# Low parts of eight weight tiles made by accumulating DMAs, three renormalisations fewer per table, and looser buffers in a hybrid SSM/attention encoder block

## The chip, the cores and the metric

One core of one Trainium2 chip runs the whole program. The metric is the device time of one execution in microseconds (us), the median of the runs. A core has five engines with queues of their own, which run in order and wait for one another by semaphores: TensorE (PE), VectorE (DVE), ScalarE (ACT), GpSimd (POOL) and SyncE (SP). DMAs are issued by SP, ACT and POOL.

## The reference

One encoder layer (DEPTH 1) over 512 tokens and 16 meta tokens, width 1024, all in float32:

```python
h = rms_norm(h_res, norm_mix_g[i])
proj = h @ w_in[i]
u, q, k, v, g_ssm, g_attn = jnp.split(proj, split_at, axis=-1)
y = s5_bidirectional(u, ...)                  # 32 groups, 64 complex states, both directions
z = jax.nn.gelu(y, approximate=False)
y_ssm = z * jax.nn.sigmoid(z @ w_glu[i] + b_glu[i])
...                                           # q, k: per-head norm and rotary; attention
merged = (jax.nn.sigmoid(g_ssm) * (y_ssm @ w_ssm_proj[i])
          + jax.nn.sigmoid(g_attn) * (y_attn @ w_attn_proj[i]))
h_res = h_res + merged @ w_out[i]
h2 = rms_norm(h_res, norm_mlp_g[i])
h_res = h_res + jnp.square(jax.nn.relu(h2 @ w_mlp_in[i])) @ w_mlp_out[i]
```

One direction of the S5 part is a complex diagonal recurrence x_t = lb x_(t-1) + B u_t, followed by Re(C x). What the change touches lies in this part and in the projections that run beside it.

## The kernel before, in words

**Precision.** Each float32 operand of a dense product is split into a high part (a copy rounded to fp32r) and a low part (the operand less its high part), and `mm3` (L157 to L161) does three matmuls: high x high (L159), low x high and high x low (L160, L161, the order depends on which side the weights are).

**Weights.** `load_w` (L107) fetches 512 KB into `wf` by a DMA on SP's queue (L112), ScalarE copies it into `wh` in two halves (L98), and the low part `wl` is made in one of two ways. Either VectorE subtracts, in two halves (L125), or, where the second entry of `W_ENG` is None, ScalarE writes the negated copy into `wl` (L122) and a DMA on GpSimd's queue adds `wf` to it (L123, `accum_op=ALU.add`). The tiles `wf`, `wh` and `wl` have two buffers each. The second way is in use before the change in the MLP stage alone.

**The state stage** runs from about 56 us to 234 us. VectorE prepares the parameters of the recurrence. Then there are eight passes of four groups each, i8 = 0 to 7 (pass 0 to pass 7 below). `ssm_build` makes the pass's matrices: the transposed input matrices (VectorE products L711 to L713 in `tmp`, PE transposes `w` L720), the output matrices `W2` (VectorE L728 to L733, two buffers), the phase table `e` from two products in `x1` and `x2` (L747) and their sum (L749), and the small Toeplitz part (PE `kt` L758, then `T0` by eight small DMAs). `ssm_run` does the pass: PE `st` (L787), ScalarE copies into `Sx` (L789, L790), on VectorE a rotation (L795 to L797), a scan (L800) and a rotation back, on ScalarE the copies into `X` (L806, L807), and PE `yo` (L813 with `T0`, L815 with `X` and `W2`). `m1` of the rotation lies in `rs1`, the same store as `x1`, so that the next pass's `x1` cannot be written before the copies into `X` have read `m1`.

**Filler.** Between the steps of the passes PE is given the matmuls of fourteen projection tasks: u columns (`t_u`, 48 matmuls of 264 columns into `ups`) and gate columns (`t_gate`, 24 matmuls of 512 columns into `gps`). Each task loads one weight tile with `load_w`, one task ahead. The first eight tiles of the stage are called load 1 (the task u1), load 2 (the gate g0), load 3 (g1) and so on. The instructions of each engine are put in order when the program is built, by a list scheduler with priorities; that order is then fixed.

**Phase tables.** `phase_tables` builds powers of the unit phase by doubling. After each squaring (`csq`) it calls `renorm`, six VectorE instructions on 128x32 values, which brings the modulus back to one.

Of the kernel before, what the change touches and what calls it, by code (L numbers as in the profile page):

```python
# [10 lines left out]
F32 = mybir.dt.float32  # L11
# [59 lines left out]
def hybrid_block(ctx, tc, x, meta, w_in, w_glu, w_ssm, w_attn, w_out, w_m1, w_m2,  # L71
# [20 lines left out]
    W_ENG = [lambda i: (S, Q if i % 2 else V)]  # L92
# [391 lines left out]
    x_st.close()  # L484
    fill_q += [kv_t[0], t_u(0, uTs), kv_t[1]]
    drain()
    W_ENG[0] = lambda i: (S, V)


    def tt(a, b, op, o=None):  # L490
# [83 lines left out]
    def csq(r, i):  # L574
        rr = tz(tz(r, r, ALU.mult), tz(i, i, ALU.mult), ALU.subtract)
        ii = stt(r, 2.0, i, ALU.mult, ALU.mult, o=ptile(ppz))
        return rr, ii

    def renorm(r, i):
        m = tz(tz(r, r, ALU.mult), tz(i, i, ALU.mult), ALU.add)  # L580
        m = ts(m, -0.5, ALU.mult, 1.5, ALU.add, o=ptile(ppz))
        return tz(r, m, ALU.mult), tz(i, m, ALU.mult)
# [7 lines left out]
    def phase_tables():  # L590
        wr, wi = wri
        phase = []
        for nb in (8, 9):
            tr_ = sp.tile([128, G, nb], F32, name=f"ph{nb}r")
            ti_ = sp.tile([128, G, nb], F32, name=f"ph{nb}i")
            V.memset(tr_[:, :, 0:1], 1.0)
            V.memset(ti_[:, :, 0:1], 0.0)
            m = 1
            while m < nb:
                n = min(m, nb - m)  # L600
                bcw = [a[:, :, None].to_broadcast([128, G, n]) for a in (wr, wi)]
                s1, s2 = [a[:, :G * n].rearrange("p (g n) -> p g n", g=G) for a in (sc5, sc6)]
                cmul(V, tr_[:, :, m:m + n], ti_[:, :, m:m + n], tr_[:, :, 0:n], ti_[:, :, 0:n], bcw[0], bcw[1], s1, s2)
                m *= 2
                if m < nb or nb == 8:
                    wr, wi = renorm(*csq(wr, wi))
            phase.append((tr_, ti_))

        (pbr, pbi), (par, pai) = phase
        pa1, pa2 = [sp.tile([128, G, 2, 9], F32, name=f"pa{j}") for j in range(2)]  # L610
        S.copy(out=pa1[:, :, 0], in_=par)
        S.copy(out=pa1[:, :, 1], in_=pai)
        S.activation(out=pa2[:, :, 0], in_=pai, func=AF.Copy, scale=-1.0)
        S.copy(out=pa2[:, :, 1], in_=par)
        return pa1, pa2, pbr, pbi
# [79 lines left out]
    def ssm_build(i8):  # L695
# [46 lines left out]
        e = sw.tile([128, 4, 2, 72], F32, tag="e", name="e")  # L742
        es = sw.tile([128, 2, 4, NC], F32, tag="es", name="es")
        E4 = [128, 4, 18, 8]
        x1, x2_ = [a.rearrange("p (g a b) -> p g a b", g=4, b=8) for a in (rs1, rs2)]
        for o, a, b_ in ((x1, pa1, pbr), (x2_, pa2, pbi)):
            V.tensor_tensor(out=o, in0=a[:, gs].rearrange("p g s a -> p g (s a)")[:, :, :, None].to_broadcast(E4),  # L747
                            in1=b_[:, gs, None, :].to_broadcast(E4), op=ALU.mult)
# [27 lines left out]
    def ssm_run(i8, ws_, Uf):  # L776
        W1T, W2, T0, er, es = ws_
        gs = slice(4 * i8, 4 * i8 + 4)
        b = i8 % 2
        SX = [128, 2, 4, NC]  # L780
        S.copy(out=dec[:, :, :, 1:], in_=m8[:, None, gs, None].to_broadcast([128, 2, 4, NC - 1]))

        Sx = sw.tile(SX, F32, tag="S", name="Sx")
        for i in range(2):
            ps = ptr("st")[:, :4 * NC].rearrange("p (g n) -> p g n", g=4)
            for g in range(4):
                own = PE.matmul(out=ps[:, g, :], lhsT=W1T[i][:, g, :], rhs=Uf[:, 4 * b + g, :], start=True, stop=True)  # L787
            anchors.append(own.ins)
            S.copy(out=Sx[:64, i], in_=ps[:64])  # L789
            S.copy(out=Sx[64:, i], in_=ps[64:, :, ::-1])  # L790
        m1, m2_ = [a[:, :8 * NC].rearrange("p (i g n) -> p i g n", i=2, g=4) for a in (rs1, rs2)]
        erb = er[:, None].to_broadcast(SX)

        def rotate(op):
            V.tensor_tensor(out=m1, in0=Sx, in1=erb, op=ALU.mult)  # L795
            V.tensor_tensor(out=m2_, in0=Sx[:, ::-1], in1=es, op=ALU.mult)
            marks[1] = V.tensor_tensor(out=m1, in0=m1, in1=m2_, op=op).ins  # L797
        fl_ = [a.rearrange("p i g n -> p (i g n)") for a in (Sx, dec, m1)]
        rotate(ALU.add)
        V.tensor_tensor_scan(out=fl_[0], data0=fl_[1], data1=fl_[2], initial=0.0, op0=ALU.mult, op1=ALU.add)  # L800
        rotate(ALU.subtract)

        xf = sw.tile(SX, F32, tag="X", bufs=XB, name="X")
        Q.memset(xf[:64, :, :, 0:1], 0.0)  # L804
        Q.memset(xf[64:, :, :, NC - 1:NC], 0.0)
        S.copy(out=xf[:64, :, :, 1:], in_=m1[:64, :, :, :NC - 1])  # L806
        S.copy(out=xf[64:, :, :, NC - 2::-1], in_=m1[64:, :, :, :NC - 1])  # L807
        Xn = [xf[:, i] for i in range(2)]
        yield

        ps = ptr("yo")[:NCR].rearrange("n (g f) -> n g f", g=4)
        for g in range(4):
            PE.matmul(out=ps[:, g, :], lhsT=Uf[:, 4 * b + g, c0:], rhs=T0[:, g, :], start=True, stop=False)  # L813
            for i in range(2):
                own = PE.matmul(out=ps[:, g, :], lhsT=Xn[i][:, g, c0:], rhs=W2[i][:, g, :], start=False, stop=i == 1)  # L815
        anchors.append(own.ins)
        marks[0] = copy_on(S, Ysb[:, :, 4 * b:4 * b + 4, :], ps.rearrange("n g (t p) -> n t g p", t=T)).ins
# [760 lines left out]
```

## Time and profile before

| | |
|---|---|
| median of 3 runs | 918.15 us (916.77 to 918.69) |
| profiled execution | 916.32 us, its span 914.6 us |
| busy, share of the span | PE 93%, DVE 76%, ACT 56%, POOL 20% |
| mean granted TensorE clock | 0.976 |
| chain that ended last | PE 76%, DVE 14%, ACT 5% |
| accumulating DMAs | 27, all after 590 us |

Times are microseconds from the start of the span. A row of the timeline gives start, duration, engine, line, operation, output and inputs, and in brackets how long the engine had been idle before it and who released it. Instructions of one engine overlap a little at their ends, so what one costs is the distance to the next start. The granted clock is a share of 2.4 GHz; the lower of its two levels is 1.2 GHz.

### The profile page before, as it was taken

The numbers are of one execution on the slowest core, as the hardware profiler recorded it, in microseconds if no ns is written. First come the engines' busy times: TensorE is split into PE (matmuls) and PEld (weight loads), VectorE is DVE, ScalarE is ACT, GpSimd is POOL, SyncE is SP. The second block draws the span as 40 slices with busy tenths as digits, with TensorE's granted clock in tenths as the row PEclk, the third lists the DMA queues.
The fourth block names the chain that finished last, engine by engine and source line by source line (L and its number), as shares of the span: only waits on it lengthen the run. The fifth ranks groups of instructions, "written<-read, shape, count | busy, mean of one in ns | idle before, by whom it ended". The sixth has DMA issues, their size and how long they took to land.

```text
span 914.6 us, 13094 instructions
## 1 busy us (share of the span) xinstructions
PE 852.6 (93%) x4798; PEld 729.8 (80%) x4798; DVE 691.2 (76%) x1263; ACT 515.9 (56%) x908; POOL 184.4 (20%) x177
## 2 busy tenths in 40 slices
PE   6999789998999899899989999999999999999994
PEld 5998677776887789788878888888888888888884
DVE  6999999878879687867685536747667666776687
ACT  5444465555663656578785335565655555555543
POOL 1000000000111476657644432010010001000000
PEclk9999899899999999999999999999999999999997
DMA  7222202222113110002014343565656566565402
GB/s 236 71 67 67 75 13 63 75 58 65 63 47 95 50 47 24 24 24 70 2 48 137 115 138 92 187 161 138 183 138 161 140 181 153 147 180 127 109 1 92
DMA packets 96322, 88.33 MB, mean 97 GB/s; under 512 B 4337, under 2 KB 79665, under 8 KB 96258
## 3 DMA queue, kind: packets, MB, share of 16 engines
q1 hardware_dynamic: 87824, 69.25, 25.2%
q0 software_dynamic: 4016, 14.21, 7.9%
q10 hardware_dynamic: 4418, 4.04, 1.6%
q8 instruction: 38, 0.62, 0.3%
q14 instruction: 26, 0.21, 0.1%
HBM read 69.03 MB, written 2.10 MB: 78 GB/s over the span
## 4 chain that ended last, share of the span: by engine, by line
PE 76%; DVE 14%; ACT 5%; issue 2%; DMA 1%; POOL 1%; DVEq 0%; ACTq 0%; POOLq 0%
PE m L161 6%; PE m L160 6%; PE m L159 6%; PE o L159 5%; PE o L160 5%; PE o L161 5%; PE pv L1173 3%; PE sc L1099 2%; PE atr L1123 2%; DVE wl L125 2%; PE adp L159 2%; PE adp L160 2%; PE adp L161 2%; PE gps L159 2%; PE kt L758 2%
## 5 line engine op out<-in xcount | busy, mean ns | idle before, releaser
L98 ACT CAST wh<-wf 128x512 fp32r<-128x512 f32 (+1 forms) x120 | 89.8, 778 | 94.5 <-PE m L160 58.2
L1444 DVE TENSOR_TENSOR ybuf<-o,ybuf 128x1024 f32<-128x1024 f32 x52 | 63.5, 1221 | 67.9 <-PE o L161 67.8
L161 PE MATMUL m<-h2h,wl 128*128 128x512 f32 (+1 forms) x272 | 102.4, 377 | 0.8 <-DVE wl L125 0.8
L160 PE MATMUL m<-h2l,wh 128*128 128x512 f32 (+1 forms) x272 | 102.5, 377 | 0.2 <-DVE h2l L103 0.2
L159 PE MATMUL m<-h2h,wh 128*128 128x512 f32 (+1 forms) x272 | 102.3, 377 | 0.3 <-ACT h2h L98 0.2
L160 PE MATMUL o<-ol,fh 128*128 128x512 f32 (+1 forms) x216 | 83.2, 385 | 0.0
L159 PE MATMUL o<-oh,fh 128*128 128x512 f32 (+1 forms) x216 | 83.2, 385 | 0.0
L161 PE MATMUL o<-oh,fl 128*128 128x512 f32 (+1 forms) x216 | 83.2, 385 | 0.0
L125 DVE TENSOR_TENSOR wl<-wf,wh 128x512 fp32r<-128x512 f32 (+1 forms) x81 | 69.2, 873 | 14.1 <-ACT wh L98 13.3
L123 POOL DMA_DIRECT2D wl<-wf x27 | 23.4, 866 | 279.0 <-ACT wl L122 262.3
L161 PEld LDWEIGHTS m<-h2h,wl 128*128 128x128 f32 x272 | 51.2, 188 | 10.6 <-DVE wl L125 1.3
L159 PEld LDWEIGHTS m<-h2h,wh 128*128 128x128 f32 x272 | 51.1, 188 | 10.1 <-ACT h2h L98 0.5
L160 PEld LDWEIGHTS m<-h2l,wh 128*128 128x128 f32 x272 | 51.2, 188 | 9.7 <-DVE h2l L103 0.4
L1103 DVE TENSOR_REDUCE mx<-sc 128x1 f32<-128x528 f32 x64 | 44.7, 701 | 11.7 <-PE sc L1099 10.8
L103 DVE TENSOR_TENSOR pl<-atr,ph 128x512 fp32r<-128x512 f32 x64 | 43.4, 683 | 9.3 <-ACT ph L98 8.5
L98 ACT CAST ph<-atr 128x512 fp32r<-128x512 f32 x64 | 37.1, 584 | 18.1 <-PE atr L1123 17.5
L161 PEld LDWEIGHTS o<-oh,fl 128*128 128x128 f32 x216 | 40.6, 188 | 8.2
L159 PEld LDWEIGHTS o<-oh,fh 128*128 128x128 f32 x216 | 40.6, 188 | 8.1
L160 PEld LDWEIGHTS o<-ol,fh 128*128 128x128 f32 x216 | 40.6, 188 | 7.9
L804 POOL MEMSET X<- 64x8 f32 x8 | 0.9, 112 | 218.4 <-PE yo L815 218.4
L1113 POOL TENSOR_TENSOR ea<-zT,rsm 128x528 f32<-128x528 f32 x32 | 34.2, 1069 | 21.4 <-DVE rsm L1112 19.3
L1123 PE MATMUL atr<-ident,ea 128*128 128x128 f32 x192 | 36.0, 281 | 0.7 <-DVE pl L103 0.6
(403 smaller groups left out, 2523.4 us busy)
## 6 DMA issues: line engine op xcount, KB each, us to landing
wf<-in_w_in_dram SPq DMA_DIRECT2D x32, 512.0 KB, 3.9
wf<-in_w_m_dram SPq DMA_DIRECT2D x32, 512.0 KB, 4.1
q<-in_w_m_dram SPq DMA_DIRECT2D x32, 512.0 KB, 4.5
wl<-wf POOLq DMA_DIRECT2D x27, 512.0 KB, 4.4
ybuf<-in_x_dram SPq DMA_DIRECT2D x8, 512.0 KB, 3.9
wf<-in_w_attn_dram SPq DMA_DIRECT2D x8, 512.0 KB, 3.9
wf<-in_w_out_dram SPq DMA_DIRECT2D x8, 512.0 KB, 3.3
wf<-in_w_ssm_dram SPq DMA_DIRECT2D x4, 512.0 KB, 3.4
```

Of the source, the lines that this page charges most:

```text
L98: return S.copy(out=o, in_=i)
L103: b = el.tensor_tensor(out=l, in0=src, in1=h.bitcast(F32), op=ALU.subtract)
L123: Q.dma_start(out=wl[:, r], in_=wf[:, r], accum_op=ALU.add)
L125: el.tensor_tensor(out=wl[:, r], in0=wf[:, r], in1=wh[:, r].bitcast(F32), op=ALU.subtract)
L159: PE.matmul(out=o, lhsT=lh, rhs=rh, start=first, stop=False, skip_group_check=goes_on)
L160: PE.matmul(out=o, lhsT=lh, rhs=rl, start=False, stop=False, skip_group_check=goes_on)
L161: return PE.matmul(out=o, lhsT=ll, rhs=rh, start=False, stop=last, skip_group_check=goes_on)
L1103: g0 = V.tensor_reduce(out=mx, in_=sc[:, :, :NL], axis=AX.XY, op=ALU.max, negate=True)
L1113: pend.append(lambda: Q.tensor_tensor(out=en, in0=e, in1=rs_.to_broadcast([128, L]), op=ALU.mult))
L1123: PE.transpose(ps[:, j * 256 + q * 128:j * 256 + q * 128 + 128], ea[2 * f + q][:, c:c + 128], ident)
L1173: PE.matmul(out=pvt[0][:, 256 * f:256 * f + 256], lhsT=vw, rhs=pw, start=left == [8, 9], stop=left == [0, 0])
L1444: V.tensor_tensor(out=x2q[r][h], in0=z, in1=x2q[r][h], op=ALU.add)
```

## The change

It has four parts. The low parts of the state stage's first eight weight tiles are made by ScalarE's negated copy and an accumulating DMA, no longer by VectorE. `renorm` is called once, at the end of the first phase table, where it was called after each of six squarings: five calls go. `x1` moves from `rs1` to a free part of `yfl`. `Sx` gets two buffers.

```diff
-    W_ENG[0] = lambda i: (S, V)
+    nw0 = wcount[0]
+    W_ENG[0] = lambda i: (S, V if i - nw0 > 7 else None)
...
-                    wr, wi = renorm(*csq(wr, wi))
+                    wr, wi = csq(wr, wi)
+                    if m == nb:
+                        wr, wi = renorm(wr, wi)
...
-        x1, x2_ = [a.rearrange("p (g a b) -> p g a b", g=4, b=8) for a in (rs1, rs2)]
+        x1, x2_ = [a.rearrange("p (g a b) -> p g a b", g=4, b=8) for a in (yfl[:, 3072:3648], rs2)]
...
-        Sx = sw.tile(SX, F32, tag="S", name="Sx")
+        Sx = sw.tile(SX, F32, tag="S", bufs=2, name="Sx")
```

From `nw0` on the changed kernel's line numbers are one larger, from the `renorm` lines on three larger.

The scheduler puts the instructions in another order. At the start of the stage, where load 1 becomes the weights of the task u1 (`ups`), PE has this before:

```order
L161 MATMUL kvps<-wh,hTl 16x256
L159 MATMUL ups<-hTh,wh 128x264
L160 MATMUL ups<-hTl,wh 128x264
L159 MATMUL ups<-hTh,wh 128x264
L160 MATMUL ups<-hTl,wh 128x264
L161 MATMUL ups<-hTh,wl 128x264
```

And in the changed kernel:

```order
L161 MATMUL kvps<-wh,hTl 16x256
L159 MATMUL ups<-hTh,wh 128x264
L160 MATMUL ups<-hTl,wh 128x264
L159 MATMUL ups<-hTh,wh 128x264
L160 MATMUL ups<-hTl,wh 128x264
L723 MATMUL w_922<-ident,ybuf 128x128 x4
L161 MATMUL ups<-hTh,wl 128x264
```

Four transposes of pass 0 now stand ahead of the first matmul that reads the low part `wl`; before they came 27 matmuls later. ScalarE has this at the same place before (`kvps` is the K/V task that ends there):

```order
L98 COPY kvraw<-kvps 128x256 x2
L98 CAST wh<-wf 128x512 x2
L98 COPY kvraw<-kvps 16x256
L98 CAST wh<-wf 128x512 x2
L721 COPY W_921<-w_922 128x512
```

And in the changed kernel, where the negated copies of loads 1 and 2 stand ahead of their high parts:

```order
L98 COPY kvraw<-kvps 128x256 x2
L122 ACTIVATE wl<-wf 128x1024
L98 CAST wh<-wf 128x512 x2
L122 ACTIVATE wl<-wf 128x1024
L98 COPY kvraw<-kvps 16x256
L98 CAST wh<-wf 128x512 x2
L724 COPY W_921<-w_922 128x512
```

On GpSimd, whose queue held only the zeroing of the edges of `X` in this stage, the accumulating DMAs come in between. This is the piece of the changed kernel from pass 0's zeroing to pass 2's:

```order
L123 DMA wl<-wf 128x1024
L807 MEMSET X 64x8
L808 MEMSET X 64x8
L123 DMA wl<-wf 128x1024 x6
L807 MEMSET X 64x8
L808 MEMSET X 64x8
L123 DMA wl<-wf 128x1024
```

Loads 2 to 7 stand between pass 0's zeroing and pass 1's, load 8 behind pass 1's.

The third place is on VectorE, from the end of pass 2's rotation back (its last product into `gbuf` is the first row) to pass 3's scan. Before:

```order
L797 TENSOR_TENSOR gbuf<-gbuf,rs_888 128x528
L747 TENSOR_TENSOR rs_888<-pa_1116,ph8i 128x576
L747 TENSOR_TENSOR gbuf<-pa_1115,ph8r 128x576
L749 TENSOR_TENSOR e<-gbuf,rs_888 128x576
L731 TENSOR_TENSOR W_1853<-ybuf 128x512
L795 TENSOR_TENSOR gbuf<-Sx,e 128x528
L728 TENSOR_TENSOR ybuf<-Cr,PA_848 128x512
L729 TENSOR_TENSOR ybuf<-Ci,PA_847 128x512
L125 TENSOR_TENSOR wl<-wf,wh 128x512
```

The second half of pass 3's rotation and the second half of the subtraction follow, then more of the next build, and the scan only as the seventh row from there. In the changed kernel:

```order
L800 TENSOR_TENSOR gbuf<-gbuf,rs_888 128x528
L750 TENSOR_TENSOR rs_888<-pa_1056,ph8i 128x576
L752 TENSOR_TENSOR e<-ybuf,rs_888 128x576
L750 TENSOR_TENSOR ybuf<-pa_1055,ph8r 128x576
L798 TENSOR_TENSOR gbuf<-Sx,e 128x528
L799 TENSOR_TENSOR rs_888<-Sx,es 128x528
L800 TENSOR_TENSOR gbuf<-gbuf,rs_888 128x528
L734 TENSOR_TENSOR W_1793<-ybuf 128x512
L125 TENSOR_TENSOR wl<-wf,wh 128x512
L803 SCALAR_TENSOR_TENSOR Sx<-dec,gbuf 128x528
```

One of the two products of the phase table (`x1`, now in `ybuf`) is already made when pass 2 ends, and pass 3 is rotated at once and scanned two instructions later, where products of the next build came in between before.

## Rows read from the trace of the kernel before

**Rows 1.** Stretches of the state stage: length, busy time of each engine (instructions), clock, DMA share.

```profile
60.00:80.00 20.00, 20.00 (x123) 17.05 (x122) 19.88 (x52) 8.12 (x18) 0.00 (x0) 1.00 0.35 94
...
104.00:112.00 8.00, 1.28 (x5) 0.72 (x5) 6.55 (x10) 4.39 (x10) 0.00 (x0) 0.65 0.23 66
112.00:118.00 6.00, 5.25 (x27) 4.66 (x26) 5.75 (x9) 1.94 (x4) 0.21 (x2) 0.62 0.00 0
```

**Rows 2.** Who PE waited for between 95 and 235 us: total, times, longest.

```profile
PE yo L815 <- ACT X L807: 6.6, 3, 3.5
```

**Rows 3.** PE's timeline at the outputs of passes 0, 1, 3, 7, and the stage's end.

```profile
109.45 0.69 PE L813 MATMUL yo<-T,Uf 128*64 128x128 f32 x2 [5.27 <-ACT Sx L790]
111.60 1.09 PE L815 MATMUL yo<-W,X 128*64 128x128 f32 x4 [1.46 <-ACT X L807]
...
123.10 0.60 PE L815 MATMUL yo<-W,X 128*64 128x128 f32 x4
...
159.43 0.71 PE L678 MATMUL ug<-ident,Vc 66*128 66x66 f32 x8 [2.13 <-ACT Vc L98]
161.81 1.09 PE L815 MATMUL yo<-W,X 128*64 128x128 f32 x4 [1.67 <-ACT X L807]
...
228.76 0.65 PE L815 MATMUL yo<-W,X 128*64 128x128 f32 x4 [3.52 <-ACT X L807]
...
229.63 1.06 PE L815 MATMUL yo<-W,X 128*64 128x128 f32 x4
...
234.32 0.50 PE L159 MATMUL adp<-zh,wh 128*128 128x512 f32 x1
```

**Rows 4.** The subtractions of the first eight loads on DVE, 56 to 107 us.

```profile
L125 DVE TENSOR_TENSOR wl<-wf,wh x16: 679/682/693, 56.1 to 105.4; 128x512 fp32r<-128x512 f32 x16
```

**Rows 5.** DVE's timeline: a renorm instruction and its successor, a subtraction and its successor.

```profile
47.89 0.18 DVE L492 TENSOR_TENSOR p<-p 128x32 f32<-128x32 f32 x1
47.99 0.68 DVE L563 TENSOR_TENSOR sc<-p,Bi 128x512 f32<-128x512 f32 x1
...
59.43 0.68 DVE L125 TENSOR_TENSOR wl<-wf,wh 128x512 fp32r<-128x512 f32 x1
60.03 0.68 DVE L711 TENSOR_TENSOR ybuf<-LBi,PA 128x512 f32<-128x512 f32 x1
```

**Rows 6.** The group of x1, 60 to 240 us: busy, mean ns, idle before and releaser.

```profile
L747 DVE TENSOR_TENSOR gbuf<-pa,ph8r 128x576 f32<-128x576 f32 x8 | 6.0, 755 | 4.2 <-ACT X L807 4.2
```

**Rows 7.** The accumulating DMAs of the MLP stage, their landing, the first with its copy.

```profile
L123 POOL DMA_DIRECT2D wl<-wf x27: 860/862/917, 600.6 to 856.0; - x27
DMA to landing us min/median/max: 4.4/4.4/5.7
599.21 1.05 ACT L122 ACTIVATE wl<-wf 128x1024 fp32r<-128x1024 f32 x1
600.57 0.92 POOL L123 DMA_DIRECT2D wl<-wf  x1 [46.09 <-ACT wl L122]
```

**Rows 8.** The start of the stage on ACT and PE, and the first gate matmul.

```profile
54.57 1.14 ACT L98 CAST wh<-wf 128x512 fp32r<-128x512 f32 x2 [1.03 <-PE kvps L161]
56.82 0.39 PE L161 MATMUL ups<-hTh,wl 128*128 128x264 f32 x1
60.33 0.60 PE L720 MATMUL w<-ident,ybuf 128*128 128x128 f32 x4
64.55 0.50 PE L159 MATMUL gps<-hTh,wh 128*128 128x512 f32 x1
```

**Rows 9.** DVE: pass 0's first phase product, the K norm's reduction, pass 7's last rotation step.

```profile
100.53 0.75 DVE L747 TENSOR_TENSOR gbuf<-pa,ph8r 128x576 f32<-128x576 f32 x1
...
202.73 1.49 DVE L917 TENSOR_REDUCE st<-ybuf 128x20 f32<-128x1280 f32 x1 [1.34 <-ACT ybuf L916]
...
226.54 0.70 DVE L797 TENSOR_TENSOR gbuf<-gbuf,rs 128x528 f32<-128x528 f32 x1
```

**Rows 10.** A DMA issue of T0 on ACT's queue: shortest, median, longest.

```profile
L769 ACTq DMA_DIRECT2D T<-gbuf x32: 592/608/1437, 77.3 to 210.1; - x32
```

## The prediction, made before the changed kernel was run

> **What bounds the kernel now.** I read the table of stretches first. Over the whole span PE is busy 93%, so a change pays only where PE stands still or runs at its lower clock. In the state stage both kinds occur. From 60 to 80 us PE and DVE are both full [rows 1]. From 104 to 112 us PE works 1.28 of 8 us, and up to 118 us its granted clock is near 0.62, while DVE is busy 12.3 of these 14 us [rows 1]: the filler has run out and PE waits for pass 0's chain on DVE. The list of PE's waits has 6.6 us in three waits for `X` [rows 2]; ahead of the first of them stand 5.27 us until `Sx` is copied (the copy waits on ACT's queue behind work that waits for DVE). The timeline puts them at passes 0, 3 and 7, and shows the price of the lower clock: a step of four `yo` matmuls takes 1.09 us at 111.60 and 161.81 us and 0.60 us at 123.10 us [rows 3]. A whole `yo` has four such steps, 4 x (1.09 - 0.60) = 2.0 us, so the low level costs it 2.0 us, and a little more with the `T0` matmuls in between.
>
> So DVE bounds the stage in several places and PE in others, above all from 60 to 104 us. DVE work that goes is worth at most PE's idle time; anything that holds PE between 56 and 104 us costs in full.
>
> **What goes.** The sixteen subtractions lie between 56.1 and 105.4 us [rows 4]. One costs 0.60 us, from its start to the next [rows 5]: 16 x 0.60 = 9.6 us. Five `renorm` calls are 30 instructions at 0.10 us [rows 5]: 3.0 us. Both lie ahead of or in pass 0's chain, whose phase product starts at 100.53 us [rows 9]. `x1` in its own store removes DVE's 4.2 us of waiting for the copies into `X` [rows 6]. Two buffers of `Sx` let ACT copy the next pass's input before the rotation back has read the last one. Together DVE gets 9.6 + 3.0 + 4.2 = 16.8 us.
>
> What PE gets from it, place by place:
> - Pass 0: the waits of 5.27 and 1.46 us [rows 3]. DVE reaches the chain about 12 us earlier, more than the 6.7 us, so both go; with PE kept busy `yo` runs at the high level, 2.0 us less, which I round up to 2.3 for the `T0` matmuls. Together 9.0.
> - Pass 3: waits of 2.13 and 1.67 us, and `yo` at the low level from 161.81 us, 2.0: 5.8. The order now rotates pass 3's input (copied early into the second `Sx`) ahead of the next build's products, so I take all of it.
> - Pass 7: 3.52 us, and behind it three of the four steps at the low level (1.06 us at 229.63 us, [rows 3]), 1.5: 5.0. The chain from pass 6's `st` to pass 7's last rotation step at 226.54 us [rows 9] loses little, and the K norm's reduction of 1.49 us [rows 9], which stood in a hole of DVE, now stands inside it, since its square is written over the store that `x1` takes. I take half: 2.5.
>
> The sum is 17.3 us, which agrees with DVE's 16.8. The tasks' matmuls are neither more nor fewer, so whatever filler moves keeps its price.
>
> **What comes in.** Eight negated copies of 1.05 us on ACT [rows 7], which is busy 8.12 of 20 us at 60 to 80 us [rows 1], so their busy time is hidden. Eight DMA issues of 0.86 us on POOL, which is idle there. What counts is how long `wl` takes. From the copy's start: 1.05, then 0.31 until the DMA is issued (599.21 + 1.05 to 600.57 us), then 4.4 to landing [rows 7]: 5.8 us, where the subtraction took 1.3.
>
> - Load 1. The buffer is free when the K/V task ends; ACT's first copy was released at 54.57 us [rows 8]. So `wl` is there at 54.5 + 5.8 = 60.3 us. PE took the first low part at 56.82 us [rows 8]; the four transposes that now stand ahead of it cover at most their 0.60 us [rows 8], I take 0.5. PE stalls for 60.3 - 57.3 = 3.0 us, in the stretch where it is the bound. Pass 0's `kt` and its successors come no later than before, as they now stand ahead of the first gate task.
> - The clock behind that stall. PE lost the high level behind waits of 3.52 us and of 5.27 + 1.46 us [rows 3]; the price was 1.5 and 2.0 to 2.3 us. Behind 3.0 us it lies between 0 and 2.3; I take 1.5, near the upper end, because 3.0 is close to 3.52.
> - Loads 2 to 8. A buffer is freed when its task ends, and PE then has the other task to do. From 64.55 us [rows 8] to the idle before 109.45 us, that is 104.2 us [rows 3], PE does 102 gate matmuls and 48 of `ups` (its order before, from the first `gps` to the first `yo` with `X`), 5.25 tasks, in 39.6 us: 7.5 us each. That covers 5.8 us with 1.7 to spare, provided that ACT is free. It is not always: in the new order load 4's copy stands behind four DMA issues of `T0`, 0.6 us each [rows 10], so I expect about 1 us there and 0.5 elsewhere: 1.5 (bounds 0 and 7 x 3.0 = 21).
> - On POOL pass 1's zeroing stands behind the DMA of load 7. By the walk above that DMA is issued near 106 us and the zeroing needs pass 0's `yo` anyway, so it is covered; a later load 7 would hold pass 1's `X` by as much.
> - DVE now runs ahead and meets another wait: pass 2's `W2` needs the buffer that pass 0's `yo` reads. Behind that instruction pass 1's scan is queued, and PE's next `yo` waits for it with what filler is left. I take 1.0 on PE; the bounds are 0 and the longest wait for `X` now, 3.52 us [rows 3].
>
> Costs: 3.0 + 1.5 + 1.5 + 1.0 = 7.0. Net gain 17.3 - 7.0 = 10.3 us. The profiled execution of 916.32 us (span 914.6) becomes 906.0 (span 904.3). It is 1.83 us under the median of the runs, so the median goes from 918.15 to 907.8 us.
>
> **A rule against it.** The 27 landings of the MLP stage lie between 4.4 and 5.7 us, median 4.4, although DVE works there beside them [rows 7]. The state stage's DVE is fuller (19.88 of 20 us, [rows 1]). The Trainium skill's page "SBUF — State Buffer" (section on the two separate sides, the box on DVE blocking a DMA) says that a DMA issued from GpSimd has its descriptors written by GpSimd, and that VectorE locks it out while it runs an instruction in a two-port performance mode, for which an fp32 copy from SBUF to SBUF is the example. By that rule landings would be late only beside such copies; DVE's work between 56 and 106 us is nearly all tensor_tensor products, the kind that ran beside the landings of 4.4 us. If DVE did hold the DMAs, each would take the longest landing, 5.7 - 4.4 = 1.3 us more, and with no cover 8 x 1.3 = 10.4 us would use up the gain: 918.
>
> **The rivals.**
> 1. Slower: `wl` is late for every load. It decides when ACT starts the negated copy more than 1.7 us after the buffer is free, on the mean of the eight. For it: ACT's queue is in order, and copies that wait for PE or DVE and the `T0` issues stand ahead. Against it: ACT is busy 8 of 20 us there [rows 1]. Price: 8 x 3.0 = 24 in place of 4.5, the rest as above: 24 + 1.5 + 1.0 - 17.3 = 9 us slower, 927.
> 2. The gain stays at pass 0: later waits keep their length because DVE is tied to PE by the two buffers of `W2` and by the single `X`. Then 9.0 - 7.0 = 2 us, 916. For it: POOL's and DVE's instructions for `X` and `W2` wait for `yo`, so no pass can run far ahead. Against it: the order at pass 3 has the rotation ahead of the build's products.
> 3. The rule above holds: 918.
> 4. All covers hold: 17.3 - 3.0 and the rest of pass 7, 2.5: 17 us faster, 901.
>
> **How the numbers follow.** Forecast (6 to 15 us faster, 903 to 912): 0.63. Rival 1: 0.13. Rival 2: 0.17. Rival 3: 0.04. Rival 4: 0.03. What a measurement here can tell from no change is about 0.2%, 1.8 us, near the spread of the three runs. Rival 2 lies at that edge, I give it 0.11 faster and 0.06 same; rival 3 is 0.01 same and 0.03 slower. So faster 0.63 + 0.11 + 0.03 = 0.77, same 0.07, slower 0.16. The range 900 to 920 leaves out most of rival 1 and little else. The forecast's own is 903 to 912.
>
> **What would show it.** Right: a PE wait near 57 us of about 3 us whose releaser is the DMA of `wl`; none of the waits of [rows 3] at passes 0 and 3; clock 1.00 around pass 0's `yo`, which starts near 107 us (111.6 before); landings of L123 near 4.4 us in this stage too; the stage's end (the first `adp` matmul, 234.3 us before) near 224. Wrong: PE waits for `wl` or L123 before every task up to 110 us; landings over 5.7 us; pass 1's `X` held by its zeroing; or, with the early waits gone, the same wait found again at passes 5 to 7.

## The result, and the profile after

The changed kernel takes 905.3 us (median of four runs, 902.95 to 906.97) against 917.9 us for the kernel before in the same runs: a ratio of 0.9862, 95% interval 0.9836 to 0.9887, 12.6 us faster. The profiled execution took 902.95 us with a span of 901.0 us, 13.6 us less than before. (Of the five `renorm` calls that go, two lie in the first phase table and three in the second, so the title's "three per table" holds for the second alone.) Here are PE's waits in it between 45 and 240 us (total, times, longest).

```profile
PE kt L761 <- DVE W L736: 3.9, 2, 2.2
PE yo L818 <- ACT X L810: 1.7, 1, 1.7
PE ups L161 <- DMA wl<-wf: 1.6, 1, 1.6
PE yt L827 <- ACT gbuf L98: 1.5, 2, 0.8
PE kt L761 <- DVE W L734: 1.2, 3, 0.6
PE ups L159 <- ACT kvraw L98: 1.2, 1, 1.2
PE ug L681 <- ACT Vc L98: 1.1, 2, 0.7
PE gps L161 <- DMA wl<-wf: 0.8, 2, 0.5
```

Three waits for `X` with 6.6 us [rows 2] have become one of 1.7. PE's timeline puts them in place, with the same points as [rows 3] and load 1 ahead.

```profile
57.80 0.39 PE L159 MATMUL ups<-hTh,wh 128*128 128x264 f32 x1 [1.22 <-ACT kvraw L98]
60.33 0.39 PE L161 MATMUL ups<-hTh,wl 128*128 128x264 f32 x1 [1.58 <-DMA wl<-wf]
...
106.03 0.65 PE L818 MATMUL yo<-W,X 128*64 128x128 f32 x4
...
151.19 0.65 PE L818 MATMUL yo<-W,X 128*64 128x128 f32 x4
...
186.55 1.73 PE L761 MATMUL kt<-W,BP 128*48 128x128 f32 x14 [2.22 <-DVE W L736]
...
217.41 0.62 PE L818 MATMUL yo<-W,X 128*64 128x128 f32 x4 [1.73 <-ACT X L810]
...
221.31 0.50 PE L159 MATMUL adp<-zh,wh 128*128 128x512 f32 x1
```

The first `adp` matmul comes 13.0 us earlier than in [rows 3], so all but 0.6 of the 13.6 us lie in the state stage. Passes 0 and 3 begin without a wait and at the high level (0.65 us a step); load 1 stalls PE, and two `kt` groups wait for `W2` near 187 and 193 us.

**A ledger of the stage.** Time that PE loses is idle time, and of its busy time the share that the granted clock takes (1 less PEclk). The stretches of the stage in the kernel before (start and end, length, busy time with instructions of PE, PEld, DVE, ACT and POOL, PEclk, DMA share, GB/s):

```profile
54.00:82.00 28.00, 27.79 (x178) 23.80 (x176) 27.83 (x75) 11.73 (x25) 0.00 (x0) 1.00 0.33 85
82.00:138.00 56.00, 46.78 (x311) 40.20 (x309) 51.62 (x126) 32.79 (x68) 0.43 (x4) 0.91 0.18 48
138.00:166.00 28.00, 24.13 (x162) 21.30 (x162) 24.65 (x40) 14.58 (x33) 0.21 (x2) 0.91 0.29 75
...
166.00:234.32 68.32, 61.51 (x372) 51.34 (x370) 57.37 (x97) 37.88 (x75) 0.85 (x8) 0.94 0.22 62
```

And in the changed kernel:

```profile
54.00:82.00 28.00, 25.02 (x164) 21.58 (x163) 26.92 (x81) 15.16 (x29) 3.74 (x6) 1.00 0.55 123
82.00:138.00 56.00, 53.38 (x375) 46.10 (x374) 46.20 (x80) 39.85 (x81) 3.86 (x8) 1.00 0.51 116
138.00:166.00 28.00, 27.58 (x169) 22.36 (x168) 23.86 (x39) 15.52 (x34) 0.43 (x4) 0.94 0.29 77
166.00:221.31 55.31, 48.07 (x316) 40.05 (x314) 47.09 (x77) 32.94 (x66) 0.66 (x6) 1.00 0.20 53
```

Idle time is length less PE's busy time. The clock's share was added up in steps of 1 us, because much of the low clock lies in idle time and costs nothing there: 8.9 us before, 1.7 after. (In the third stretch after, for example, 27.58 us at 0.94 is 1.7.) In us lost:

| stretch | before: idle, clock | after: idle, clock | gained |
|---|---|---|---|
| load 1, 54 to 82 | 0.2, 0 | 3.0, 0 | -2.8 |
| passes 0 and 1, 82 to 138 | 9.2, 2.7 | 2.6, 0 | 9.3 |
| passes 2 and 3, 138 to 166 | 3.9, 2.1 | 0.4, 1.7 | 3.9 |
| 166 to the stage's end | 6.8, 4.1 | 7.2, 0 | 3.7 |
| sum | 20.1, 8.9 | 13.3, 1.7 | 14.0 |

Stage end less 54 us and less both losses is 151.3 us before and 152.3 after, and 150.0 to 152.7 in all fourteen kernels below: PE's own work differs by 2.7 us at most, and how long a kernel's stage is follows from what PE loses in it. The stretches are fixed in time, and the changed kernel is 6 us ahead at pass 2 and 11 at pass 3, so a loss near a border can fall into another one.

### The profile page after: what moved, and what is told of

Same layout as the page of the kernel before. It is cut to its first block, busy times and chain, and to the rows that moved or that the text cites. A ratio compares the mean times of both kernels' runs of the same rounds, so it can differ in the third digit from the quotient of the medians.

```text
span 901.0 us, 13081 instructions
## 1 busy us (share of the span) xinstructions
PE 844.8 (94%) x4798; PEld 721.6 (80%) x4798; DVE 676.2 (75%) x1217; ACT 521.9 (58%) x916; POOL 193.2 (21%) x185
## 4 chain that ended last, share of the span: by engine, by line
PE 74%; DVE 14%; ACT 6%; DMA 3%; issue 3%; POOL 1%; DVEq 0%; ACTq 0%; POOLq 0%; SPq 0%
PE m L161 6%; PE m L160 6%; PE m L159 6%; PE o L161 5%; PE o L159 5%; PE o L160 5%; PE pv L1176 3%; PE sc L1102 2%; PE atr L1126 2%; DVE wl L125 2%; PE gps L159 2%; PE gps L161 2%; PE gps L160 2%; PE adp L159 2%; PE adp L160 2%
## 5 line engine op out<-in xcount | busy, mean ns | idle before, releaser
L123 POOL DMA_DIRECT2D wl<-wf x35 | 30.3, 865 | 377.4 <-ACT wl L122 299.5
L125 DVE TENSOR_TENSOR wl<-wf,wh 128x512 fp32r<-128x512 f32 (+1 forms) x65 | 57.3, 900 | 13.4 <-ACT wh L98 13.2
L161 PEld LDWEIGHTS m<-h2h,wl 128*128 128x128 f32 x272 | 51.2, 188 | 10.5 <-DVE wl L125 1.3
L159 PEld LDWEIGHTS m<-h2h,wh 128*128 128x128 f32 x272 | 51.1, 188 | 10.1 <-ACT h2h L98 0.5
L1106 DVE TENSOR_REDUCE mx<-sc 128x1 f32<-128x528 f32 x64 | 44.8, 702 | 12.7 <-PE sc L1102 11.9
L98 ACT CAST ph<-atr 128x512 fp32r<-128x512 f32 x64 | 37.1, 584 | 18.1 <-PE atr L1126 17.6
L122 ACT ACTIVATE wl<-wf 128x1024 fp32r<-128x1024 f32 x35 | 36.8, 1050 | 0.9 <-PE kvps L160 0.9
L1176 PE MATMUL pv<-ph,Vhl 128*128 128x256 f32 x128 | 34.6, 294 | 2.2 <-ACT ybuf L1148 1.4
```

The lines of the kernel that those rows point to most:

```text
L98: return S.copy(out=o, in_=i)
L122: S.activation(out=wl[:, r], in_=wf[:, r], func=AF.Copy, scale=-1.0)
L123: Q.dma_start(out=wl[:, r], in_=wf[:, r], accum_op=ALU.add)
L125: el.tensor_tensor(out=wl[:, r], in0=wf[:, r], in1=wh[:, r].bitcast(F32), op=ALU.subtract)
L159: PE.matmul(out=o, lhsT=lh, rhs=rh, start=first, stop=False, skip_group_check=goes_on)
L161: return PE.matmul(out=o, lhsT=ll, rhs=rh, start=False, stop=last, skip_group_check=goes_on)
```

## The experiments

Each is timed beside the kernel before; ratios with 95% intervals. "Start" is pass 0's first matmul on `X`, the losses are the ledger's, all from the profiled execution. A difference in us is the ratio's, on the time of the kernel before. Each edit lets the scheduler put the whole stage in order anew, so a run differs from its partner in the order of the instructions too; no run holds that order fixed.

| kernel | ratio | start | idle | clock | stage end |
|---|---|---|---|---|---|
| before | 1 | 111.60 | 20.1 | 8.9 | 234.32 |
| the change | 0.9862 (0.9836 to 0.9887) | 106.03 | 13.3 | 1.7 | 221.31 |
| DMA part alone | 1.0049 (1.0023 to 1.0074) | 107.76 | 22.3 | 9.6 | 237.41 |
| renorm part alone | 0.9959 (0.9943 to 0.9976) | 108.87 | 18.9 | 9.2 | 232.72 |
| all but the DMA part | 0.9907 (0.9883 to 0.9932) | 108.80 | 13.8 | 5.0 | 224.95 |
| DMA and renorm parts | 0.9870 (0.9838 to 0.9902) | 102.74 | 13.4 | 1.7 | 221.42 |
| DMA alone, six loads | 1.0019 (0.9997 to 1.0041) | 108.88 | 20.9 | 9.1 | 235.38 |
| change, idle subtractions | 0.9976 (0.9961 to 0.9990) | 114.25 | 17.6 | 10.1 | 233.72 |
| change, load 1 by VectorE | 0.9894 (0.9869 to 0.9918) | 104.62 | 12.6 | 4.6 | 221.87 |
| DMA and renorm, load 1 by VectorE | 0.9903 (0.9884 to 0.9923) | 103.88 | 14.9 | 6.2 | 226.88 |
| change, fourteen loads | 0.9907 (0.9882 to 0.9931) | 106.84 | 13.9 | 3.4 | 223.96 |
| three W2, shared scratch | 1.0297 (1.0270 to 1.0324) | 100.02 | 38.3 | 13.2 | 257.14 |
| the same, load 1 by VectorE | 1.0189 (1.0156 to 1.0222) | 95.38 | 33.0 | 12.0 | 250.18 |
| three W2, one Sx | 0.9864 (0.9842 to 0.9887) | 109.75 | 12.5 | 6.9 | 223.44 |

### The parts, one by one

All but the DMA part (in the change):

```diff
-    W_ENG[0] = lambda i: (S, V if i - nw0 > 7 else None)
+    W_ENG[0] = lambda i: (S, V)
```

> The change without its DMA part: VectorE again makes all low parts, the other three parts stay. Theory (freed VectorE time is what moves pass 0, and the subtractions are most of it): pass 0 is still late, its gain is only the 3.0 us of the renorm part; passes 3 and 7 keep their gains (5.4 and 3.3 us measured in the change), and the costs of the late low parts (3.0 + 0.8 us) go. Net gain 3.0 + 5.4 + 3.3 - 1.8 (waits for W2) = 10 us, about 908 us, 1 to 4 us slower than the change; a wait for X of 3 to 5 us stays at pass 0. Rival A (the low parts were not what held pass 0, the other three parts do it all): pass 0 starts near 104 us with no wait, and without load 1's stall the time is 901 to 902 us, below the change. Rival B (passes 3 and 7 gained from the freed subtractions too): 912 us or more.

The DMA part alone (in the kernel before):

```diff
-    W_ENG[0] = lambda i: (S, V)
+    nw0 = wcount[0]
+    W_ENG[0] = lambda i: (S, V if i - nw0 > 7 else None)
```

> Before with the DMA part alone. Theory: the 9.6 us taken off VectorE are more than the 6.7 us by which pass 0 was late, so pass 0 gains 9.0 us; load 1 costs 3.0 and the later loads 0.8 us; passes 3 and 7 keep their waits. Net gain 5.2 us, about 912.7 us (911 to 915). Rival A (the other three parts do it all): slower than before by the 3.8 us of late low parts, about 921.7 us. Rival B (the subtractions loosen the later passes as well): 907 us or less.

The renorm part alone (in the kernel before):

```diff
-                    wr, wi = renorm(*csq(wr, wi))
+                    wr, wi = csq(wr, wi)
+                    if m == nb:
+                        wr, wi = renorm(wr, wi)
```

> Before with the renorm part alone (the phase products leave out five of the renormalisations, as in the change). Theory: 30 instructions of 0.10 us ahead of pass 0's chain, 3.0 us off VectorE, which is busy without a break there, so pass 0's wait shrinks by 3.0 us: about 914.9 us (913.5 to 916.5). Rival A (pass 0 is held by something else than VectorE's amount of work, such as ScalarE's queue): no change, 917.9 us. Rival B: the 3.0 us also carry PE over its lower clock at pass 0: 912.5 us or less.

DMA and renorm parts, without the other two (in the change):

```diff
-        x1, x2_ = [... for a in (yfl[:, 3072:3648], rs2)]
+        x1, x2_ = [... for a in (rs1, rs2)]
-        Sx = sw.tile(SX, F32, tag="S", bufs=2, name="Sx")
+        Sx = sw.tile(SX, F32, tag="S", name="Sx")
```

> The change without the x1 store and without the second Sx buffer (low parts by DMA and the renorm part alone). Theory: pass 0 keeps its 9.0 us, load 1 costs its 3.0 us, and the waits at passes 3 and 7 come back (5.4 and 3.3 us, less the 1.8 us of waits for W2, which VectorE then reaches later): about 912 us, 6 to 7 us slower than the change. Rival A (the x1 store and the second Sx buffer are slack, VectorE's freed time does it all): 905 us, as the change. Rival B (the two are also needed at pass 0): 915 us or more, with a wait for X at pass 0.

On 916.3 us the four measured -8.5, +4.5, -3.7 and -11.9 us. The first and third come near the theory in time (-10 and -3 expected), but not in place: the first has no wait for `X` left at pass 0, and the third is near by luck. In the renorm part alone pass 0's waits do shrink by 3.0 us (from 6.7 to 3.7), but pass 1 gets a new one of 5.60 us, so that passes 0 and 1 lose 15.2 us where they lost 11.9 before; the gain lies behind 138 us, where pass 7 has no wait for `X` any more.

```profile
108.87 0.62 PE L817 MATMUL yo<-W,X 128*64 128x128 f32 x4 [1.72 <-ACT X L809]
...
124.70 1.08 PE L817 MATMUL yo<-W,X 128*64 128x128 f32 x4 [5.60 <-ACT X L809]
```

The other two go against the theory. The `x1` store and the second `Sx` buffer are worth nothing in sum beside the other two parts (rival A), though without the DMA part they bring 0.9959 to 0.9907. And the DMA part alone loses (by the medians 2.8 us; three of its twelve executions, at 926 to 928 us, make the 4.5), although pass 0 starts 3.8 us earlier and without a wait. Its timeline on PE shows where that is given back: the clock falls behind load 1's stall (a `ups` step of 0.22 us in place of 0.12), load 7 is late, and pass 1 waits.

```profile
60.54 0.39 PE L161 MATMUL ups<-hTh,wl 128*128 128x264 f32 x1 [2.02 <-DMA wl<-wf]
...
62.00 0.42 PE L161 MATMUL ups<-hTh,wl 128*128 128x264 f32 x1
62.22 0.42 PE L159 MATMUL ups<-hTh,wh 128*128 128x264 f32 x1
...
115.00 0.50 PE L161 MATMUL gps<-hTh,wl 128*128 128x512 f32 x1 [2.38 <-DMA wl<-wf]
...
127.07 1.08 PE L816 MATMUL yo<-W,X 128*64 128x128 f32 x4 [4.08 <-ACT X L808]
```

### Is it load 7? Six loads by DMA

```diff
+    W_ENG[0] = lambda i: (S, V if i - nw0 > 5 else None)
```

> Before with the DMA part alone, for six loads instead of eight; VectorE subtracts again for loads 7 and 8. It is to explain why the DMA part alone lost 4.5 us although pass 0 came 3.8 us earlier. Theory (load 7's negated copy stood on ScalarE behind the copies into pass 0's X, which wait for VectorE; its low part came 2.4 us late at 115 us, the kt matmuls behind it too, and pass 1's scan stands on VectorE behind an addition that needs kt, so pass 1's X came 4.1 us late and the clock fell): the wait for wl at 115 us goes, pass 1's wait for X falls under 2 us, and the time to 912 to 914 us, 5 us below the run with eight. Rival A (pass 1's chain is late because VectorE has too much to do): 2.4 us more work on VectorE, the wait of pass 1 stays, 917 us or more. Rival B (load 1's stall and the low clock behind it are the loss): nothing changes there, 917 to 919 us.

917.07 us, not to be told from before: the wait for `wl` at 115 us is gone and pass 1 waits longer still, 5.63 us at 124.96 us. The theory of the late load 7 fell, and rival A's place and time hold: VectorE is late at pass 1. Two things make it late. One is a hole in pass 0's chain, shown by ScalarE's and VectorE's timelines, here of the run with the DMA part alone, first ScalarE:

```profile
94.02 1.14 ACT L98 CAST wh<-wf 128x512 fp32r<-128x512 f32 x2 [3.09 <-DMA wf<-in_w_in_dram]
...
97.34 0.44 ACT L753 ACTIVATE es<-e 128x264 f32<-128x264 f32 x1
```

```profile
97.82 0.71 DVE L797 TENSOR_TENSOR rs<-Sx,es 128x528 f32<-128x528 f32 x1 [4.24 <-ACT es L753]
```

ScalarE's cast for a later load waits 3.09 us for that load's `wf`, the copies of `es` stand behind it, and VectorE idles 4.24 us inside pass 0's chain (4.08 us with six loads). `wf` is late because its buffer is now released by the accumulating DMA and no longer by a subtraction; SP's waits between 55 and 110 us say so, first in the kernel before and then in the changed one (9.2 us more in seven waits):

```profile
SPq L112 <- DVE wl L125: 47.9, 7, 14.9
```

```profile
SPq L112 <- DMA wl<-wf: 57.1, 7, 17.7
```

The change has the same hole:

```profile
96.19 0.71 DVE L799 TENSOR_TENSOR rs<-Sx,es 128x528 f32<-128x528 f32 x1 [4.59 <-ACT es L755]
```

It has no wait for `X` at pass 1 all the same, so the hole alone does not make that wait.

With the DMA and renorm parts together `es` was placed ahead of that cast, and the hole is gone:

```profile
88.95 0.42 ACT L755 ACTIVATE es<-e 128x264 f32<-128x264 f32 x1
92.07 1.14 ACT L98 CAST wh<-wf 128x512 fp32r<-128x512 f32 x2 [2.70 <-DMA wf<-in_w_in_dram]
```

Pass 1's scan then starts at 106.48 us where the run with six loads has it at 116.98. Of these 10.5 us, 6.4 are there when pass 1's rotation starts (103.90 against 110.31 us). The other 4.1 come between rotation and scan, and they are the second thing, the order on VectorE. The kernel before has nothing between but the rest of the rotation; with six loads the scheduler put three subtractions and five instructions of the next build there; in the renorm part alone, without any of the DMA part, five such instructions, the first behind a wait for a buffer of `W2`. The three in this order:

```profile
113.07 0.71 DVE L795 TENSOR_TENSOR gbuf<-Sx,e 128x528 f32<-128x528 f32 x1
...
115.38 1.26 DVE L800 TENSOR_TENSOR_SCAN Sx<-dec,gbuf 128x528 f32<-128x528 f32 x1
```

```profile
110.31 0.70 DVE L796 TENSOR_TENSOR gbuf<-Sx,e 128x528 f32<-128x528 f32 x1
...
116.98 1.25 DVE L801 TENSOR_TENSOR_SCAN Sx<-dec,gbuf 128x528 f32<-128x528 f32 x1
```

```profile
110.34 0.71 DVE L797 TENSOR_TENSOR gbuf<-Sx,e 128x528 f32<-128x528 f32 x1
112.46 0.69 DVE L733 TENSOR_TENSOR W<-ybuf 128x512 f32<-128x512 f32 x1 [1.41 <-PE yo L817]
...
116.71 1.26 DVE L802 TENSOR_TENSOR_SCAN Sx<-dec,gbuf 128x528 f32<-128x528 f32 x1
```

The run with the DMA part alone has eleven instructions between. These three, with five or more, wait 4.1 to 5.6 us for `X` at pass 1; the change with two, and the DMA and renorm parts with one, don't wait. (The run with three `W2` and one `Sx`, below, has ten between; PE's wait there, 5.0 us, is for a copy on ScalarE.) So a part alone may be worth less than beside the others because of the order that it gets; how much is order and how much VectorE's time these runs don't separate.

### Is it VectorE's time at all?

The change, with the subtractions still done into a spare store that nobody reads:

```diff
                 Q.dma_start(out=wl[:, r], in_=wf[:, r], accum_op=ALU.add)
+                if dmy:
+                    for r_ in (slice(0, 4), slice(4, 8)):
+                        V.tensor_tensor(out=dmy[0], in0=wf[:, r_], in1=wh[:, r_].bitcast(F32), op=ALU.subtract)
...
+    dmy.append(sw.tile([128, 4, 128], F32, tag="dmy", name="dmy"))
```

> The change with the two subtractions of each of the eight loads still done by VectorE, but into a store that nobody reads; the low parts that TensorE takes come from the accumulating DMA. So VectorE has the load of before and the DMA's costs are paid as well. Theory (the DMA part earns by VectorE's freed time alone): the time of the run without the DMA part, 907.6 us, and the stalls at load 1 and behind it (3.0 + 0.8 us) on top: about 911 us, 5 to 6 us slower than the change. Rival A (the other parts leave VectorE enough slack, its freed time is worth nothing by now): 905 us. Rival B (the late start of the gates makes the chain wait as well): 914 us or more.

0.9976, 913.97 us: 10.4 of the change's 12.6 us are lost again (1.0 less 0.9976 leaves 2.2 us), and PE's timeline has the waits for `X` at passes 0 and 1, with the low clock:

```profile
114.25 1.09 PE L822 MATMUL yo<-W,X 128*64 128x128 f32 x4 [1.89 <-ACT X L814]
...
128.68 1.09 PE L822 MATMUL yo<-W,X 128*64 128x128 f32 x4 [3.35 <-ACT X L814]
```

The theory's place is right; its size was 3 us short, and the value lies on rival B's bound. The run adds more than VectorE's time. The idle subtractions read `wh` and stand in VectorE's queue, which runs in order, so VectorE also waits for ScalarE's casts (between 54 and 125 us):

```profile
DVE dmy L127 <- ACT wh L98: 4.3, 4, 1.9
```

Pass 0's rotation starts at 104.64 us where the change has it at 90.22, 14.4 us later, though sixteen subtractions cost 9.6. The clock also fell behind load 1 (2.8 us). So the run shows that the change's gain goes when VectorE is held up again, but not that freed time alone makes it.

### Load 1 without its stall

```diff
+    W_ENG[0] = lambda i: (S, None if 0 < i - nw0 <= 7 else V)
```

> The change, but VectorE makes the low part of load 1 by its two subtractions again; loads 2 to 8 keep the DMA. Theory (load 1's stall of 1.22 + 1.58 us near 58 us costs in full, because TensorE is the bound there): 2.8 us less stall, and 1.2 us more work on VectorE, which has 9 us of idle time before pass 0's chain in the change: 2 to 3 us faster than the change, about 902.5 us, with pass 0's first matmul on X near 104 us instead of 106. Rival A (what TensorE does earlier it waits for later, since pass 0's chain on VectorE decides): no difference, 905 us, with a wait for X at pass 0. Rival B (landing of load 1 disturbs the neighbours too): more than 4 us faster.

> The change without the x1 store and the second Sx buffer, and with load 1's low part by VectorE. Without the first two alone pass 0 began at 102.7 us and the time was as the change's. Theory (what came back in the run with load 1 by VectorE was the order that it got, T0's matmuls waiting near 97 us, not VectorE's 1.2 us): if the order here has no such wait, the stall of 2.8 us is won in full, 901 us. Rival A (a stall taken away near 58 us is waited for again later, since VectorE's chains decide): 904 to 907 us, with new waits on TensorE of 3 us or more before pass 4.

Neither is faster than the same kernel with the stall: 0.9894 and 0.9903 against 0.9862 and 0.9870. PE has no wait from 56 to 62 us, but then one of 1.0 us for ScalarE, and the stretch to 82 us loses 1.4 and 1.5 us in place of 3.0. Pass 0 starts 1.4 us earlier in the first and 1.1 later in the second. The first loses the gain near 97 us, in waits for `T0` and for ScalarE with a low clock behind them, and at pass 3 (waits of 1.85 and 1.50 us at 153 to 156 us); in the second PE's timeline has these waits:

```profile
98.68 0.59 PE L159 MATMUL ups<-hTh,wh 128*128 128x264 f32 x1 [2.76 <-ACT t L366]
...
153.30 0.71 PE L681 MATMUL ug<-ident,Vc 66*128 66x66 f32 x8 [2.19 <-ACT Vc L98]
155.64 0.62 PE L818 MATMUL yo<-W,X 128*64 128x128 f32 x4 [1.62 <-ACT X L810]
...
221.45 1.09 PE L818 MATMUL yo<-W,X 128*64 128x128 f32 x4 [3.53 <-ACT X L810]
```

It has no wait for `T0` near 97 us and is slow all the same, so the theory that the order of `T0`'s matmuls took the first one's gain fell, and rival A's main point holds in both: what PE no longer waits for near 58 us it waits for later, though in the first not at pass 0, where rival A had it. The edit also moves filler between the passes, and these runs don't separate that from the chains on VectorE.

### Fourteen loads

```diff
+    W_ENG[0] = lambda i: (S, V if i - nw0 > 13 else None)
```

> The change with the accumulating DMA for the state stage's first fourteen loads instead of eight. Six more loads take 7.2 us off VectorE in passes 1 to 7. Theory (after pass 1 TensorE has filler to cover a low part that comes 4.5 us later, and VectorE's time still counts at kt and at pass 7): 1 to 3 us faster than the change, 902 us. Rival A (VectorE has time to spare there): no difference, 904 us. Rival B (negated copies stand behind copies into X on ScalarE, low parts come late as in the run with the DMA part alone): 907 us or more, with waits for wl of over 1 us behind pass 1.

0.9907, 907.3 us, rival B's time, but behind pass 1 only one wait for `wl` is over 1 us (1.09 us at 212.03 us). Its losses lie elsewhere: one `kt` still waits, 1.71 us at 192.03 us, with the low clock behind it (1.65 us), and pass 7 waits 2.78 us in place of 1.73. Six more subtractions off VectorE bring nothing.

### A third buffer of W2

Two buffers hold pass 4's and 5's `kt`. First with the scratch store of the rotation moved to make room, alone and with load 1 by VectorE, then with the room taken from the second `Sx` buffer:

```diff
-            w2 = sw.tile(W4, F32, tag=f"W2{im}", bufs=2, name="W2")
+            w2 = sw.tile(W4, F32, tag=f"W2{im}", bufs=3, name="W2")
-    rs1, rs2 = gfl[:, 1536:2112], sp.tile([128, 576], F32, name="rs2")
+    rs1, rs2 = gfl[:, 1536:2112], yfl[:, 0:576]
```

> The change with three buffers of W2 instead of two (the rotation's second scratch store moves into the free part of ybuf to make the room). Theory (VectorE may not write a build's W2 before the yo two passes earlier has read its buffer, so the kt matmuls wait 5.1 us in all behind passes 0 to 5): the waits of kt for W2 fall under 1.5 us and the time by 3 to 4 us, about 902 us. Rival A (kt waits because VectorE has too much to do, not for the buffer): the waits stay or turn up as waits for X, 905 us. Rival B (VectorE runs ahead with the builds and its in-order queue then delays the rotations): slower, 907 us or more.

> Both of the two: three buffers of W2, and VectorE makes load 1's low part. Theory: the two stalls lie at different places (58 us, and passes 4 to 6) and both cost TensorE in full, so their gains add: 5 to 7 us faster than the change, about 899 us. Rival A (VectorE or the filler becomes the bound once one of them is gone): the gain of the better one alone, about 902 us. Rival B (neither helps): 905 us.

```diff
-            w2 = sw.tile(W4, F32, tag=f"W2{im}", bufs=2, name="W2")
+            w2 = sw.tile(W4, F32, tag=f"W2{im}", bufs=3, name="W2")
-        Sx = sw.tile(SX, F32, tag="S", bufs=2, name="Sx")
+        Sx = sw.tile(SX, F32, tag="S", name="Sx")
```

> Three buffers of W2 again, but with the room taken from the second Sx buffer instead of moving the rotation's scratch store, since the run with three lost 38 us and changed both. Theory (the scratch store was the fault: shared with the builds' products, a rotation and a build can no longer be interleaved on VectorE): with its own store again the loss goes, the waits of kt for W2 go, 900 to 903 us. Rival A (the third buffer is the fault: builds run ahead and the rotations stand behind them in VectorE's queue): 930 us or more, with waits for X of 5 us as before. Rival B (neither does anything once the store is back): 904 us.

The first two change two things at once: 943.59 and 934.24 us, 38 and 29 us more than the change. With the scratch store left alone the time is the change's, 903.25 us (0.9864). So the shared store, alone or with the second `Sx` buffer beside three of `W2`, made the loss, and not the third buffer by itself. In the first VectorE waits 25.7 us for the input of its rotations:

```profile
DVE gbuf L798 <- ACT Sx L793: 25.7, 7, 7.9
```

Why the input comes so late there stays open. In the third no `kt` waits for `W2` any more (5.1 us in the change), which fits that the two buffers held them, but one wait of 5.0 us and the clock (6.9 us in place of 1.7) took it back:

```profile
PE ug L681 <- ACT Vc L98: 5.0, 1, 5.0
PE yo L818 <- ACT X L810: 3.1, 2, 2.8
```

No version beat the change: the third buffer and the two parts without the `x1` store and the second `Sx` equal it within their intervals.

## Why the prediction was right, point by point

The forecast was 10.3 us faster, 907.8; measured were 12.6 and 905.3. The signs and the main term were right. By place the terms were off by 1.7 to 2.2 us each, three in one direction and pass 3 in the other, so that a part of the errors cancels, by luck. That DVE's 16.8 us agreed with PE's 17.3 says little: 4.2 of it are DVE's waits that the `x1` store removes, and without that store and the second `Sx` the time is the same.

- **Pass 0, 9.0 us.** Right. Both waits of [rows 3] are gone, `yo` starts at 106.03 us (about 107 was said) at the high level, and the stretch gained 9.3 us net of the later loads' waits. The runs without the DMA part (8.6 us lost in this stretch, 2.6 in the change) and with idle subtractions (14.8) bear out that VectorE's time counts here. But the step from VectorE's 12 us to PE's gain depends on the order that the edit gets: it left out the hole of 4.59 us at `es` that the later `wf` makes, and that the DMA part and the renorm part alone each give pass 0's gain back at pass 1, where their order has other instructions ahead of the scan.
- **Pass 3, 5.8 us.** Too large. Its waits went, but the clock fell just behind this pass (the 1.7 us of the third stretch), so 3.9 us came. The reason named, the new order with the second `Sx` buffer, is borne out in this stretch: without that buffer and the `x1` store it loses 5.1 us (2.6 of it in waits at 146 to 150 us), with them 2.1; without the DMA part it is 4.3 and 0.4. But the sum took no cost for them elsewhere: beside the DMA part, passes 0 and 1 lose 0.1 us without them and 2.6 with them, and the time is the same.
- **Pass 7, 2.5 us.** The wait fell from 3.52 to 1.73 us and no low clock followed, 1.8 + 1.5 = 3.3 us.
- **Load 1, 3.0 us.** Right as a stall: 1.22 + 1.58 us with `wl` at 60.33 us (60.3 was said), the ledger's 2.8. The 1.22 had another releaser than was said, the copy of `kvraw`, which now stands behind load 2's negated copy on ScalarE. As a cost of the change the stall was not shown: two runs without it gained nothing. With three `W2` and the shared scratch the same edit gained 9 us, in another order.
- **The clock behind it, 1.5 us.** Not paid in the profiled execution; paid with 1.6 to 2.8 us in five of the seven other kernels that have the stall.
- **Loads 2 to 8, 1.5 us.** 0.8 us, in two waits. Landings between 50 and 120 us had a median of 4.9 and a longest of 6.2 us, where 4.4 was taken and over 5.7 was named as a sign of being wrong; no wait behind load 1 was over 0.5 us. VectorE's load alone does not set the landing: load 1's took 4.5 us with VectorE busy 6.00 of the 6 us from 55 us, and the 6.2 us came at 85 to 91 us, where it was busy 2.97 of 6. The rule weighed against the change (the Trainium skill, "SBUF — State Buffer", the two separate sides) is that VectorE, while it runs something like an fp32 copy within SBUF, keeps GpSimd from writing descriptors. No run here tests it: VectorE's copies end at 54.7 us, and the first of these DMAs is issued at 55.82.
- **W2, 1.0 us.** The waits for `W2` grew from 3.4 us to 5.1, so 1.7, and most of them behind passes 4 and 5 instead of at pass 2.

Place by place against the ledger, which has 14.0 us where the sum had 10.3: load 1 with its clock was put at -4.5 and is -2.8; pass 0 less the later loads 7.5, and is 9.3; pass 3 5.8, and is 3.9; pass 7 less the waits for `W2` 1.5, and is 3.7. The last is larger because of the clock before: of its 4.1 us behind 166 us, 1.7 are pass 7's, but 0.7 are the end of pass 3's fall, to 168 us, and 1.7 lie behind the wait of `kt` at 201.45 us. The sum left these 2.4 us out. Rival 4 (all covers hold, 901) lies 4 us below the median, and its covers did not all hold: later loads were waited for 0.8 us and `W2` 5.1. Something like rival 2 (the gain stays at pass 0) is what the DMA part and the renorm part do alone: what pass 0 gains, pass 1 loses.

## What to carry to other kernels

Work taken off an engine with queues of dependent passes is worth only what the next late thing leaves: here two parts together gave 12 us, where one alone lost 4.5 and the other won 3.7. Where a scheduler puts the program in order, an edit also changes the order: before a difference is put down to the edit, compare what stands between the steps of the chain. When a subtraction is replaced by an accumulating DMA, count the buffers that it reads as well as the one that it writes: here the source was released only when the DMA had landed (SP waited 57.1 us for that), and whatever stands behind the next load on an in-order engine waits with it. When an experiment needs room, take it from something that was shown to be slack, not from a store that two chains will share. And an idle copy of the work that was taken away puts back its waits as well as its time.

## What was not expected of the hardware

**The same stall did or did not cost the clock.** The change and the run with three clean buffers have the same two waits at load 1 (1.22 + 1.58 and 1.22 + 1.59 us). Behind them, 60 to 65 us, first of the change and then of the other:

```profile
60.00:65.00 5.00, 4.67 (x38) 4.67 (x39) 5.00 (x14) 0.38 (x1) 0.00 (x0) 1.00 0.96 209
```

```profile
60.00:65.00 5.00, 4.93 (x22) 4.93 (x23) 5.00 (x15) 0.00 (x0) 0.00 (x0) 0.50 0.95 205
```

One runs at 2.4 GHz, the other at 1.2, and does 22 matmuls in place of 38. Of the five kernels with these two waits (to 0.02 us), three kept the clock and two lost it. The Trainium skill (page "TensorE: Matmul & The Clock Gate", Part 1) says that the chip's window for this runs free of the kernel. That would fit; no run here tests it.

**The clock also fell without a long wait.** Behind pass 3 of the change PE's waits between 140 and 157 us were 0.42 us at most, and from 157.3 to 160.8 us it ran at the low level (0.42 us from one `gps` matmul to the next, 0.23 at the high level):

```profile
154.23 0.71 PE L681 MATMUL ug<-ident,Vc 66*128 66x66 f32 x8 [0.42 <-ACT Vc L98]
...
158.32 0.63 PE L161 MATMUL gps<-hTh,wl 128*128 128x512 f32 x1
158.74 0.63 PE L159 MATMUL gps<-hTh,wh 128*128 128x512 f32 x1
```

The prediction counted the clock's price only behind waits of 3 us and more in all.

**The spread of the change's runs goes with the clock.** Its four executions have spans of 901.0, 902.7, 904.0 and 905.0 us at mean granted clocks of 0.991, 0.989, 0.987 and 0.985: 0.002 less clock is 1.0 to 1.7 us more. The profiled one is the fastest of the four, so its 1.7 us of clock loss is probably less than the usual.
